# Attention of block 1 in row groups, a recurrence staged across its heads, wider one-hot operations, and moved fills in block 2

## The chip, the cores and the metric

The kernel runs on one core of a Trainium2 chip. The metric is the device time of one execution in microseconds (us). A core has TensorE (PE in the profile, with its weight loads as PEld), VectorE (DVE), ScalarE (ACT), GpSimd (POOL) and the DMA queues, which run beside each other and wait for each other by semaphores.

## What is computed

Two transformer blocks on 512 tokens of width 1024, in float32. Block 1 has a sliding-window attention of 8 heads, a gated linear recurrence (HGRN2) of 4 heads in chunks of 32 tokens, and a PEER layer that picks 16 of 16384 experts per token and head. Block 2 has sparse and latent attention. What the change touches is this much of the reference:

```python
# attention of block 1: window 128, with the block before; one sink logit per head
s = einsum(q, k) * scale - slopes * dist
p = softmax(concatenate([s, sink]))[..., :-1]
o = einsum(p, v)

# recurrence: f = lower_bound + (1 - lower_bound) * sigmoid(f_logit), k = 1 - f
b = cumsum(log(f), axis=2)                   # inside a chunk of 32 tokens
q_dec, k_inv = q * exp(b), k * exp(-b)
o_intra = einsum(where(causal, q_dec @ k_inv, 0), v)
ds = einsum("bnshd,bnshv->bnhdv", k * exp(b_last - b), v)
state = exp(b_last) * state + ds             # chunk after chunk
o_inter = einsum(q_dec, state_before)
o = rms_norm(o_intra + o_inter, g) * silu(hg)

# PEER: two top-16 lists of 128 keys each, the best 16 of their sums, softmax over those
idx = i1 * 128 + i2;  gates = softmax(best)
out = sum over (head, slot) of gate * gelu(u[idx] . h) * v[idx]
```

## The kernel before

Activations lie with the feature on the partitions and 512 tokens in the columns (NT = 4 tiles of 128). Most projections are float32 products made of three matmuls on split operands (`mm3`, L105 to L107: high by high, and two with a low part). A column of such a projection is 8 x 3 = 24 matmuls of 128x512. Its weights arrive by DMA as `raw` and are split into `whi` (ScalarE, L68) and `wlo` (VectorE or GpSimd, L69).

Stages of block 1 are written as generators, and `weave(main, fill, per)` interleaves them: after each `yield` of the main stage it runs columns of the fill until the main stage's count is met. The tile framework then schedules the instructions of each engine by its own estimates, except under `tc.manual_schedule`, where they stay in program order.

Attention (`attention`, L358 on) takes one head at a time: a score matmul (L368; 64 rows of the array, since a head has 64 features) and a bias added by a bf16 matmul with an identity (L370) into a bank `sc`, then `softmax_pt` (VectorE maximum, ScalarE exponential, transposes L175), and the values (L375). Two heads `j` and `j + 4` lie on partitions 0 to 63 and 64 to 127. The fill, `fill_hgrn`, computes the columns q, k, v and gate of the recurrence.

The recurrence (`hgrn`, L454 on) then runs head by head: decayed products on VectorE and ScalarE (L457 to L476), scores and a transpose of the keys (L488, L494), the states of 16 chunks, the outputs (L515, L518), a norm (`hss`, `hr`, `y`) and the turn back (L531). For the states the values are copied into `vb`, which holds for each chunk of a tile its own 32 rows and zeros elsewhere, so that one 128x512 matmul (L503) makes four of them. Their running sum is a chain of 15 operations on VectorE (L507, L509). The fill, `fill_gates`, computes sixteen gate columns, and VectorE also accumulates the adaptive row for block 2 (`mod_junk`).

Behind it the columns `gh` of the two branches are joined (L550) and split for the output projection. In the PEER layer `decode` turns top-16 positions into expert indices and gates for 128 tokens at a time, almost wholly on VectorE, while TensorE already runs the first expert products (`ps_o`, L105 to L107). The three tiles behind the first then have a dense gate table built (`gate_build`): per chunk of OT = 8 tokens, one-hot rows of both index halves (`ohA`, `ohB`), the first multiplied by the gate's three bf16 parts (`ohG`), and three matmuls per token (L931).

In block 2 `fill()` gives the projections that fill its attention: `latents` with norms by a product with ones (L1535), `blocks` with two folds through DRAM (`ab`) and the compressed keys (L1587), `gates_z`, and `heads` (transposes L1633 of `qm`).

## Time and profile before

| | us |
|---|---|
| median of 3 runs (2146.77 to 2150.5) | 2150.09 |
| the profiled execution | 2153.63 |
| its span | 2151.8 |
| TensorE busy | 2039.4 (95%) |
| VectorE busy | 1568.9 (73%) |
| ScalarE busy | 883.4 (41%) |
| GpSimd busy | 495.9 (23%) |

The stages by time in the span: 

| stage | from, to | TensorE busy | VectorE busy |
|---|---|---|---|
| norm and first projections | 0 to 54.6 | 46.89 | 26.14 |
| attention of block 1 | 54.6 to 194.4 | 139.80 | 61.53 |
| recurrence | 194.4 to 359.6 | 158.94 | 121.87 |
| join, output projection | 359.6 to 417 | 51.86 | 33.09 |
| PEER scores | 417 to 560 | 142.87 | 107.63 |
| decode | 560 to 686 | 91.03 | 122.62 |
| gate build | 686 to 853 | 148.13 | 160.69 |
| experts | 853 to 1755 | 900.17 | 708.81 |
| block 2 | 1755 to 2151.8 | 359.74 | 226.57 |

A busy TensorE is not TensorE at its peak, because a matmul's record includes time in which it overlaps its neighbours. Where matmuls of different shapes follow each other, the distance from start to start tells the cost.

### The profile page before, as it was taken

What the parts mean: (1) busy time and instruction counts of PE and PEld (TensorE: products, weight loads), DVE (VectorE), ACT (ScalarE), POOL (GpSimd) and SP (SyncE); (2) the same over time, 40 slices, a digit from 0 to 9 for tenths busy, and PEclk for the clock granted to TensorE, in tenths of its full rate; (3) what the DMA queues carried; (4) which work ended last, traced back from release to release, by engine and by line L of the source; (5) the groups of instructions that cost most, each with busy time, mean ns of one, the idle gap of its engine ahead of it and who ended that gap; (6) DMA issues with size and microseconds to landing.
All of it is one profiled execution on the core that took longest, in us unless ns stands there. A gap on an engine that the chain in (4) does not pass through costs nothing.

```text
span 2151.8 us, 29889 instructions
## 1 busy us (share of the span) xinstructions
PE 2039.4 (95%) x11132; PEld 1724.6 (80%) x11132; DVE 1568.9 (73%) x3139; ACT 883.4 (41%) x1371; POOL 495.9 (23%) x408
## 2 busy tenths in 40 slices
PE   8999999999877899999999999999999999899998
PEld 6777567788776788999999999999988877677776
DVE  4446777559999899687777787888878775446556
ACT  4334434333333677333333333333334453444544
POOL 0000001220334100344444445444422001011000
PEclk9999999999988999999999999999999999899999
DMA  4213334432222555999999989999988761211012
GB/s 153 73 60 118 122 114 127 166 128 85 73 78 69 192 213 204 339 336 321 333 313 327 327 306 331 321 318 327 311 288 295 268 208 34 95 41 59 30 49 79
DMA packets 154376, 410.48 MB, mean 191 GB/s; under 512 B 13789, under 2 KB 63733, under 8 KB 150774
## 3 DMA queue, kind: packets, MB, share of 16 engines
q1 hardware_dynamic: 113332, 247.07, 34.1%
q0 software_dynamic: 37440, 136.33, 18.0%
q10 hardware_dynamic: 3458, 25.17, 3.1%
q8 instruction: 87, 1.43, 0.3%
q14 instruction: 59, 0.48, 0.1%
HBM read 378.64 MB, written 29.37 MB: 190 GB/s over the span
## 4 chain that ended last, share of the span: by engine, by line
PE 77%; DVE 16%; ACT 3%; issue 2%; POOL 1%; DMA 1%; ACTq 0%; DVEq 0%; POOLq 0%
PE ps_mm L105 13%; PE ps_mm L106 13%; PE ps_mm L107 13%; PE ps_o L105 6%; PE ps_o L107 6%; PE ps_o L106 6%; DVE ohG L911 3%; PE ps_tp L106 3%; PE ps_tp L107 3%; PE ps_tp L105 3%; PE ps_o L1325 2%; PE ps_sc L1302 2%; DVE wlo L69 2%; PE ps_tp L1318 1%; DVE ohA L908 1%
## 5 line engine op out<-in xcount | busy, mean ns | idle before, releaser
L68 ACT ACTIVATE whi<-raw 128x1024 fp32r<-128x1024 f32 (+1 forms) x363 | 382.5, 1056 | 626.0 <-issue 371.0
L69 DVE TENSOR_TENSOR wlo<-raw,whi 128x1024 fp32r<-128x1024 f32 (+1 forms) x339 | 415.8, 1229 | 183.9 <-ACT whi L68 183.4
L105 PE MATMUL ps_o<-hT_hi,whi 128*128 128x384 f32 x992 | 344.2, 347 | 18.1 <-ACT act L661 18.1
L107 PE MATMUL ps_o<-hT_hi,wlo 128*128 128x384 f32 x992 | 338.0, 341 | 7.4 <-POOL wlo L69 7.3
L106 PE MATMUL ps_o<-hT_lo,whi 128*128 128x384 f32 x992 | 337.1, 340 | 0.0
L963 POOL DMA_INDIRECT gath<-in_peer_u_dram,idx x128 | 178.7, 1396 | 369.1 <-DVE junk L971 186.0
L963 POOL DMA_INDIRECT gath<-in_peer_v_dram,idx x128 | 176.5, 1379 | 256.6 <-DVE acc L978 213.0
L105 PE MATMUL ps_mm<-hT_hi,whi 128*128 128x512 f32 (+1 forms) x544 | 224.3, 413 | 0.2 <-DVE ga L65 0.2
L107 PE MATMUL ps_mm<-hT_hi,wlo 128*128 128x512 f32 (+1 forms) x544 | 217.5, 400 | 1.0 <-DVE wlo L69 1.0
L106 PE MATMUL ps_mm<-hT_lo,whi 128*128 128x512 f32 (+1 forms) x544 | 216.9, 399 | 0.0
L105 PEld LDWEIGHTS ps_o<-hT_hi,whi 128*128 128x128 f32 x992 | 190.7, 192 | 22.7 <-ACT act L661 19.4
L107 PE MATMUL ps_mm<-whi,wl 128*128 128x512 f32 x512 | 201.2, 393 | 0.0
L106 PE MATMUL ps_mm<-wlo,wh 128*128 128x512 f32 x512 | 200.8, 392 | 0.3 <-DVE wlo L69 0.3
L105 PE MATMUL ps_mm<-whi,wh 128*128 128x512 f32 x512 | 199.4, 389 | 0.4 <-ACT wh L68 0.4
L107 PEld LDWEIGHTS ps_o<-hT_hi,wlo 128*128 128x128 f32 x992 | 190.0, 191 | 8.0 <-POOL wlo L69 7.6
L106 PEld LDWEIGHTS ps_o<-hT_lo,whi 128*128 128x128 f32 x992 | 190.4, 192 | 3.3
L978 DVE SCALAR_TENSOR_TENSOR acc<-gath,w,acc 128x1024 f32<-128x1024 f32 x127 | 162.8, 1282 | 10.4 <-DMA gath<-in_peer_v_dram,idx 8.3
L971 DVE SCALAR_TENSOR_TENSOR junk<-gath,h 128x1024 bf16<-128x1024 f32 x128 | 156.6, 1224 | 14.9 <-DMA gath<-in_peer_u_dram,idx 12.5
L933 ACT ACTIVATE gst<-ps_mm 128x512 f32<-128x512 f32 x96 | 103.4, 1127 | 47.2 <-PE ps_mm L931 45.1
L107 PEld LDWEIGHTS ps_mm<-hT_hi,wlo 128*128 128x128 f32 (+1 forms) x544 | 102.5, 188 | 23.5 <-DVE wlo L69 1.8
L106 PEld LDWEIGHTS ps_mm<-hT_lo,whi 128*128 128x128 f32 (+1 forms) x544 | 102.6, 189 | 22.2 <-issue 3.0
L105 PEld LDWEIGHTS ps_mm<-hT_hi,whi 128*128 128x128 f32 (+1 forms) x544 | 102.8, 189 | 21.1 <-issue 2.8
(482 smaller groups left out, 3611.4 us busy)
## 6 DMA issues: line engine op xcount, KB each, us to landing
raw<-in_peer_uT_dram SPq DMA_DIRECT2D x128, 512.0 KB, 5.4
raw<-in_peer_v_dram SPq DMA_DIRECT2D x128, 512.0 KB, 6.3
raw<-in_w_in_dram SPq DMA_DIRECT2D x59, 512.0 KB, 3.6
gates_dram<-gst ACTq DMA_DIRECT2D x24, 1024.0 KB, 5.4
x<-gates_dram SPq DMA_DIRECT2D x32, 768.0 KB, 9.4
raw<-in_ada_w_dram SPq DMA_DIRECT2D x24, 512.0 KB, 3.7
raw<-in_w_out_dram SPq DMA_DIRECT2D x24, 512.0 KB, 3.4
raw<-in_w_peer_q_dram SPq DMA_DIRECT2D x16, 512.0 KB, 3.6
```

The source lines that it names most:

```text
L68: self.nc.scalar.activation(hi, src, AF.Copy)
L69: (engine or self.nc.vector).tensor_tensor(lo, src, hi.bitcast(F32), op=OP.subtract)
L105: mm(out, a[0], b[0], start=start, stop=False)
L106: mm(out, a[0], b[1], start=False, stop=False)
L107: mm(out, a[1], b[0], start=False, stop=stop)
L911: nc.vector.tensor_tensor(Ag[:, i], A1, pairs(g3T[:, i, cs]), op=OP.mult)
L933: nc.scalar.activation(st[:, :, t0:t0 + 4].rearrange("p a t -> p t a"), p.rearrange("p (t a) -> p t a", t=4), AF.Copy)
L963: nc.gpsimd.indirect_dma_start(out=gath[i], out_offset=None, in_=A["peer_u" if i < NG // 2 else "peer_v"], in_offset=bass.IndirectOffsetOn ...
L971: nc.vector.scalar_tensor_tensor(junk, g, 1.0, h0, op0=OP.mult, op1=OP.mult, accum_out=act0[:, k:k + 1])
L978: nc.vector.scalar_tensor_tensor(acc0, g, w0[:, k:k + 1], acc0, op0=OP.mult, op1=OP.add)
L1302: nc.tensor.matmul(sc[i][:, :n], self.q[i], self.k[i], start=True, stop=False)
L1325: nc.tensor.matmul(self.o(i), self.pt[i][:, kb * 128:(kb + 1) * 128], self.v(i, kb), start=kb == 0, stop=kb == self.tt)
```

## The change

**Attention and its fill.** `Pair` replaces the loop over single heads: both scores stand next to each other, each head on its 64 partitions, then both bias adds; the transposes come one period later, the values one more. TensorE is in program order for the whole stage, so a fill column is an unbroken block of 24. The sigmoids of q and k and the logarithm of the decay move into `fill_hgrn`, and the transposes of `to_tok` come one column later.

```diff
+            nc.scalar.activation(lf, qh, AF.Sigmoid)
+            nc.vector.tensor_tensor(qh, qh, lf, op=OP.mult)
+            nc.scalar.activation(lf, kh, AF.Sigmoid)
             for hh in range(HG_H):
-                to_tok(P, vh[:, hh], col_f())
+                nc.vector.tensor_scalar(lf[:, hh], lf[:, hh], omlb[:, hh:hh + 1], lb[:, hh:hh + 1],
+                                        op0=OP.mult, op1=OP.add)
+                nc.vector.tensor_scalar(kh[:, hh], lf[:, hh], -1.0, 1.0, op0=OP.mult, op1=OP.add)
+            nc.scalar.activation(lf, lf, AF.Ln)
...
+            def scores(self):
+                tt, n = self.tt, self.n
+                sc = [K.bank("sc")[:, :n] for _ in range(2)]
+                for i, hh, ps_ in self.heads:
+                    nc.tensor.matmul(sc[i], qT[ps_, self.j, tt * 128:(tt + 1) * 128],
+                                     kT[ps_, self.k0 * 128:(tt + 1) * 128], start=True, stop=False)
+                for i, hh, ps_ in self.heads:
+                    nc.tensor.matmul(sc[i], K.identb, abias[:, hh, 256 - n:], start=False, stop=True)
...
+            def turn(self):
+                self.pt = []
+                for p in self.p:
+                    tp = K.bank("tp")
+                    for c in range(0, self.n, 128):
+                        nc.tensor.transpose(tp[:, c:c + 128], p[:, c:c + 128], K.ident)
+                    self.pt.append(Q.tile([128, 256], F32, name="sm_pt", bufs=4))
+                    K.copy(self.pt[-1][:, :self.n], tp[:, :self.n])
...
+            def values(self):
+                for i, hh, ps_ in self.heads:
+                    for c in range(self.n // 128):
+                        nc.tensor.matmul(self.o[:, (2 * self.j + i) * 64:(2 * self.j + i + 1) * 64],
+                                         self.pt[i][:, c * 128:(c + 1) * 128], av[:, self.k0 + c, ps_],
+                                         start=c == 0, stop=(c + 1) * 128 == self.n)
...
         def attention():
+            last = None
             for tt in range(NT):
                 o = K.bank("o")
                 for j in range(4):
-                    for g in range(2):
-                        hh = j + 4 * g
-                        ps_ = slice(g * 64, (g + 1) * 64)
-                        k0 = max(tt - 1, 0)
-                        n = (tt + 1 - k0) * 128
-                        sc = K.bank("sc")
-                        nc.tensor.matmul(sc[:, :n], qT[ps_, j, tt * 128:(tt + 1) * 128],
-                                         kT[ps_, k0 * 128:(tt + 1) * 128], start=True, stop=False)
-                        nc.tensor.matmul(sc[:, :n], K.identb, abias[:, hh, 256 - n:], start=False, stop=True)
-                        pt = K.softmax_pt(Q, sc, n, 0.125, sums[:, tt, hh:hh + 1], negm[:, tt, hh:hh + 1],
...
+                    u = Pair(tt, j, o)
+                    u.scores()
+                    yield 2.0
+                    u.turn()
+                    if last:
+                        last.values()
+                    last = u
+            last.values()
...
+        with tc.manual_schedule(engines={nc.tensor.engine}):
+            weave(attention(), fill, 2.0)
```

**The recurrence** becomes `Head` with the steps `prepare`, `scores`, `states`, `outputs` and `turn`, again with TensorE in program order and a fill column after each step; the next head's `prepare` is issued behind a head's `outputs`. The copies into `vb` go: 15 matmuls read 32 rows of `keT` and `vh` each, and write to four banks by their place in the tile. In the join the split of a column comes one column later.

```diff
-                for j in range(4):
-                    js = slice(j * CH, (j + 1) * CH)
-                    if j % 2:
-                        nc.scalar.activation(vb[js, :, j], vh[js, hh], AF.Copy)
-                    else:
-                        nc.vector.tensor_copy(vb[js, :, j], vh[js, hh])
...
+                ds = [K.bank("sc" if j < 2 else "tp") for j in range(4)]
+                for c in range(NC - 1):
+                    tt, j = divmod(c, 4)
+                    js = slice(j * CH, (j + 1) * CH)
+                    nc.tensor.matmul(ds[j][:, tt * 128:(tt + 1) * 128], keT[js, tt], vh[js, hh, tt], start=True, stop=True)
...
-                    ds = K.bank("sc")
-                    nc.tensor.matmul(ds, keT[:, tt], vb[:, tt].rearrange("p a b -> p (a b)"), start=True, stop=True)
...
+        def hgrn(yh):
+            heads = [Head(hh) for hh in range(HG_H)]
+            heads[0].prepare()
+            yield 3.0
...
+                head.scores()
...
+                head.states()
+                yield 1.0
...
+                head.outputs()
+                if after:
+                    after.prepare()
+                yield 1.0
+                head.turn(yh)
...
-                K.split(mh[0][:, c], mh[1][:, c], gh[:, c])
+                if c:
+                    K.split(mh[0][:, c - 1], mh[1][:, c - 1], gh[:, c - 1])
+        K.split(mh[0][:, c], mh[1][:, c], gh[:, c])
```

**Decode and gate build.** The slots of a tile are transposed in the middle of the next tile's top-16 work, an exponential comes later, a reduction becomes a tree of four additions, and the five one-hot operations of a chunk become two wider ones (2 and 3 rows of 1024).

```diff
+                if late and h0 == 0:
+                    turn_slots()
...
-            nc.scalar.activation(e, e, AF.Exp)
...
+            nc.scalar.activation(e, e, AF.Exp)
...
-            pk = RB.tile(kh, F32, name="pk")
-            nc.vector.tensor_reduce(pk, sum1.rearrange("p r k h -> p k h r"), axis=AX.X, op=OP.add)
+            pk = sum1[:, 0]
+            for n in (8, 4, 2, 1):
+                nc.vector.tensor_tensor(sum1[:, :n], sum1[:, :n], sum1[:, n:2 * n], op=OP.add)
...
-            nc.vector.tensor_tensor(A1, iota, pairs(i1T[:, cs]), op=OP.is_equal)
-            nc.vector.tensor_tensor(B, iota, pairs(i2T[:, cs]), op=OP.is_equal)
-            for i in range(3):
-                nc.vector.tensor_tensor(Ag[:, i], A1, pairs(g3T[:, i, cs]), op=OP.mult)
...
+            nc.vector.tensor_tensor(hot.rearrange("p c j e i -> p (c j) e i"),
+                                    iota_e[:, None].to_broadcast([128, 2 * pr, PK, 2]),
+                                    ikT[:, ch].rearrange("p c (j i) -> p (c j) i", i=2)[:, :, None]
+                                    .to_broadcast([128, 2 * pr, PK, 2]), op=OP.is_equal)
+            nc.vector.tensor_tensor(Ag, hot[:, 0:1].to_broadcast([128, 3, pr, PK, 2]),
+                                    g3T[:, ch].rearrange("p c (j i) -> p c j i", i=2)[:, :, :, None]
+                                    .to_broadcast([128, 3, pr, PK, 2]), op=OP.mult)
```

**Block 2.** The norms of the latents come behind the first fold, one z column ahead of the compressed keys, and the turn of `qm` one tile later.

```diff
+                    if kv == 0:
+                        late["norms"]()
+                        yield 1.0
+                yield from z_col(late["z"][0], 0)
...
-                    qm = T.tile([128, 4, 96], F32, name="qm", bufs=2)
+                    qm = T.tile([128, 4, 96], F32, name="qm", bufs=3)
...
-                    if len(turns) > 1:
+                    if len(turns) > 2:
```

Three places of the order of instructions follow. The first is TensorE in the attention with full windows. Before, a pair's first transposes and values are set singly between projection matmuls (`ps_mm`):

```order
L175 MATMUL ps_tp<-ident,sm_p 128x128 x2
L107 MATMUL ps_mm<-hT_hi,wlo 128x512
L175 MATMUL ps_tp<-ident,sm_p 128x128 x2
L105 MATMUL ps_mm<-hT_hi,whi 128x512
L375 MATMUL ps_o<-av,sm_pt 128x64 x2
L106 MATMUL ps_mm<-hT_lo,whi 128x512
L375 MATMUL ps_o<-av,sm_pt 128x64 x2
L107 MATMUL ps_mm<-hT_hi,wlo 128x512
L105 MATMUL ps_mm<-hT_hi,whi 128x512
```

Now one period of the stage, with the pair's work in one piece (transposes of the newest pair, values of the one before it, scores of the next):

```order
L107 MATMUL ps_mm<-hT_hi,wlo 128x512
L392 MATMUL ps_tp<-ident,sm_p 128x128 x4
L399 MATMUL ps_o<-av,sm_pt 128x64 x4
L373 MATMUL ps_sc<-kT,qT 128x256 x2
L376 LDWEIGHTS identb
L376 MATMUL ps_sc<-ga,identb 128x256
L376 LDWEIGHTS identb
L376 MATMUL ps_sc<-ga,identb 128x256
L105 MATMUL ps_mm<-hT_hi,whi 128x512
```

Transposes and values of both heads now stand together, and the projections on either side are unbroken. The second place is TensorE in the second head of the recurrence. Before, state matmuls (L503) and outputs (L515, L518) are mixed with projections:

```order
L518 MATMUL ps_o<-st,qd 32x128
L515 MATMUL ps_o<-vh,at 128x128
L503 MATMUL ps_sc<-vb,keT 128x512
L518 MATMUL ps_o<-st,qd 32x128 x2
L105 MATMUL ps_mm<-y_hi,whi 128x512
L106 MATMUL ps_mm<-y_lo,whi 128x512
L518 MATMUL ps_o<-st,qd 32x128
L107 MATMUL ps_mm<-y_hi,wlo 128x512
L518 MATMUL ps_o<-st,qd 32x128
L515 MATMUL ps_o<-vh,at 128x128
```

Now the fifteen state matmuls, alternating between two kinds of banks, follow a block of 24 projections, and the outputs follow the next block:

```order
L107 MATMUL ps_mm<-hT_hi,wlo 128x512
L543 MATMUL ps_sc<-vh,keT 128x128 x2
L543 MATMUL ps_tp<-vh,keT 128x128 x2
L543 MATMUL ps_sc<-vh,keT 128x128 x2
L543 MATMUL ps_tp<-vh,keT 128x128 x2
L543 MATMUL ps_sc<-vh,keT 128x128 x2
L543 MATMUL ps_tp<-vh,keT 128x128 x2
L543 MATMUL ps_sc<-vh,keT 128x128 x2
L543 MATMUL ps_tp<-vh,keT 128x128
L105 MATMUL ps_mm<-y_hi,whi 128x512
```

Nothing stands between the state matmuls. The third place is VectorE from the first head's sum of squares (`hss`) to its normed output `y`, for which the turn's transposes wait. Before:

```order
L524 TENSOR_REDUCE hss<-sq 128x4
L126 TENSOR_SCALAR rs_v<-hss 128x4
L69 TENSOR_TENSOR wlo<-raw,whi 128x1024
L1131 SCALAR_TENSOR_TENSOR mod_junk,mod_acc<-raw,csil 128x1024
L129 RECIPROCAL rs_r<-rs_t 128x4
L137 TENSOR_TENSOR rs_t<-rs_r 128x4
L138 TENSOR_TENSOR rs_t<-rs_t,rs_v 128x4
L139 TENSOR_SCALAR rs_t<-rs_t 128x4
L140 TENSOR_TENSOR hr<-rs_r,rs_t 128x4
L528 TENSOR_TENSOR y<-ps_o,hr 128x512
```

Now the same piece holds work of the next head:

```order
L567 TENSOR_REDUCE hss<-sq 128x4
L502 TENSOR_TENSOR qd<-qh,e 128x512
L126 TENSOR_SCALAR rs_v<-hss 128x4
L510 TENSOR_TENSOR e<-b 128x512
L506 TENSOR_TENSOR ki<-kh,e 128x512
L495 SCALAR_TENSOR_TENSOR b<-scm,lf 128x512
L129 RECIPROCAL rs_r<-rs_t 128x4
L1200 SCALAR_TENSOR_TENSOR mod_junk,mod_acc<-raw,csil 128x1024
L137 TENSOR_TENSOR rs_t<-rs_r 128x4
L138 TENSOR_TENSOR rs_t<-rs_t,rs_v 128x4
L139 TENSOR_SCALAR rs_t<-rs_t 128x4
L140 TENSOR_TENSOR hr<-rs_r,rs_t 128x4
```

and right behind these, up to the turn's output `yf`:

```order
L514 TENSOR_TENSOR ke<-kh,e 128x512
L571 TENSOR_TENSOR y<-ps_o,hr 128x512
L69 TENSOR_TENSOR wlo<-raw,whi 128x1024
L579 SCALAR_TENSOR_TENSOR yf<-ps_tp,gh_col,hgs 128x512
L69 TENSOR_TENSOR yh_lo<-yf,yh_hi 128x512
```

Behind `hss` now stand the next head's products (`qd`, `e`, `ki`, `b`, `ke`), which stood behind `yf` before.

## Rows read from the trace of the kernel before

**Rows 1.** The chain of work that ended last, shares by engine.
```profile
PE 77%; DVE 16%; ACT 3%; issue 2%; POOL 1%; DMA 1%; ACTq 0%; DVEq 0%; POOLq 0%
```

**Rows 2.** Windows: busy time and instructions of each engine, granted clock, DMA share, GB/s.
```profile
260.00:280.00 20.00, 18.18 (x67) 9.56 (x67) 14.24 (x27) 4.00 (x6) 0.00 (x0) 0.83 0.33 105
611.00:661.00 50.00, 39.13 (x193) 37.62 (x192) 48.94 (x191) 15.27 (x23) 19.28 (x8) 0.86 0.27 84
736.00:786.00 50.00, 44.77 (x477) 39.59 (x476) 50.00 (x80) 37.01 (x40) 0.00 (x0) 1.00 0.61 221
1865.00:1875.00 10.00, 7.42 (x70) 7.16 (x70) 1.69 (x5) 0.71 (x1) 0.00 (x0) 0.66 0.29 79
```

**Rows 3.** TensorE in time in block 1: start, duration, instructions; two successive pairs.
```profile
102.21 0.70 PE L368 MATMUL ps_sc<-kT,qT 64*128 64x256 f32 x2
...
110.83 0.70 PE L368 MATMUL ps_sc<-kT,qT 64*128 64x256 f32 x2
```

**Rows 4.** TensorE in time in block 2: one attention unit and its projections.
```profile
1892.99 1.00 PE L1325 MATMUL ps_o<-vn,sm_pt 128*128 128x64 f32 x8
...
1894.36 0.70 PE L1302 MATMUL ps_sc<-kn,qn 64*128 64x256 f32 x4
...
1895.09 0.48 PE L105 MATMUL ps_mm<-hT_hi,whi 128*128 128x512 f32 x1
1895.41 0.39 PE L106 MATMUL ps_mm<-hT_lo,whi 128*128 128x512 f32 x1
...
1898.63 1.00 PE L1325 MATMUL ps_o<-vn,sm_pt 128*128 128x64 f32 x8
```

**Rows 5.** Window of line 105, the first matmul of each projection trio.
```profile
194.40:359.60 165.20, 65.20 (x156) 29.48 (x156) 0.98 0.41 127
```

**Rows 6.** TensorE in time, the fourth head of the recurrence.
```profile
333.32 1.13 PE L488 MATMUL ps_sc<-qd,ki 128*128 128x128 f32 x8 [0.19 <-DVE ki L468]
...
350.55 0.38 PE L515 MATMUL ps_o<-vh,at 128*128 128x128 f32 x2
...
353.18 0.43 PE L518 MATMUL ps_o<-st,qd 128*32 128x128 f32 x8
```

**Rows 7.** VectorE by line and shape, 222 to 356: busy us, mean ns, idle.
```profile
L509 DVE SCALAR_TENSOR_TENSOR st<-st,dec,ps_sc 128x128 f32<-128x128 f32 x56 | 19.4, 346 | 1.6
...
L457 DVE TENSOR_TENSOR_SCAN b<-scm,lf 128x512 f32<-128x512 f32 x3 | 3.6, 1215 | 0.0
...
L528 DVE TENSOR_TENSOR y<-ps_o,hr 128x512 f32<-128x512 f32 x3 | 2.1, 691 | 0.1
...
L137 DVE TENSOR_TENSOR rs_t<-rs_r 128x4 f32<-128x4 f32 x3 | 0.5, 159 | 0.0
```

**Rows 8.** What TensorE waited for: us in total, times, longest.
```profile
PE ps_o L105 <- ACT act L661: 18.1, 4, 9.1
...
PE ps_tp L1633 <- DVE qm L1154: 5.9, 2, 5.1
PE ps_mm L1587 <- DMA ab<-abx: 4.8, 1, 4.8
...
PE ps_mm L105 <- DVE gh L550: 4.5, 5, 1.4
...
PE ps_tp L1535 <- ACT sq L1529: 1.8, 1, 1.8
```

**Rows 9.** VectorE by line and shape, the decode, 561 to 686.
```profile
L825 DVE TENSOR_REDUCE pk<-sum 128x128 f32<-128x2048 f32 x4 | 15.4, 3842 | 0.1
...
L846 DVE TENSOR_TENSOR ge<-ge,step 128x2048 bf16<-128x2048 bf16 x4 | 13.1, 3269 | 0.1
...
L819 DVE TENSOR_TENSOR ge<-at,row_at 128x2048 bf16<-128x2048 bf16 x4 | 4.9, 1218 | 0.0
```

**Rows 10.** VectorE in time in the gate build, a chunk from its first operation.
```profile
722.31 0.69 DVE L908 TENSOR_TENSOR ohA<-iota_e,i1T 128x1024 bf16<-128x1024 bf16 x1
...
725.32 0.69 DVE L908 TENSOR_TENSOR ohA<-iota_e,i1T 128x1024 bf16<-128x1024 bf16 x1
```

238 lines of the change are left out of this document (125 added, 113 removed).

## The prediction

> **What bounds the kernel now.** I read the chain of work that ended last first, because it says which engine an edit must relieve: TensorE carries 77% of it, VectorE 16% [rows 1]. So time saved on TensorE counts nearly everywhere. The stretches show where that fails [rows 2]: in the decode VectorE is busy 48.94 of 50 us, in the gate build all of 50.00 while TensorE has 44.77. There only VectorE work counts. Two more stretches hold idle TensorE time and a lower clock: 260 to 280 (18.18 of 20 us, clock 0.83) in the recurrence, and 1865 to 1875 (7.42 of 10, clock 0.66) in block 2. These are means over TensorE's two levels, 2.4 GHz (1.0) and 1.2 (0.5), and both follow a wait of the engine. After that I read the order of TensorE's instructions where the change moves them, and last its list of waits for what stands still.
>
> **1. Attention of block 1.** In the old order one pair of heads takes from 102.21 to the next pair's 110.83, 8.62 us [rows 3], with 24 projection matmuls. A projection matmul's step is (1898.63 - 1895.41) / 14 = 0.23 us [rows 4], so 5.52 are projections and 3.10 are the pair and the switches it causes. Block 2 already has an attention unit in the new form: values, transposes, scores side by side, masks, then an unbroken block [rows 4]. It takes 1895.09 - 1892.99 = 2.10 us, and the first matmul behind it 0.32 instead of 0.23, so 2.19. The gain of the side-by-side form can be seen in one shape: one head's two records of 64x256 last 0.70 us in all [rows 3], and two heads' four records, on two row groups, 0.70 as well [rows 4]. Block 1's bias add has 256 columns against the mask's 128, so I add 0.1: 2.29 a pair, a gain of 0.81. Twelve pairs give 9.7. For the four pairs of the first token tile, which have half the transposes and values, I take 0.6 each, 2.4. **-12 us.** Bounds: -8, if the sigmoids and the logarithm that now stand on ScalarE among the softmaxes make TensorE wait; -14, if the switch costs vanish wholly. Those gates cost TensorE nothing as long as a pair's softmax has the 5.5 us block as cover.
>
> **2. Recurrence.** The stretch 194.4 to 359.6 lasts 165.2 us and holds 156 first matmuls of projections [rows 5], so 468 with the other two of each trio, or 107.6 us at 0.23. The other 57.6 are the heads' own matmuls, switches and stalls. What a head needs in unbroken form: its scores and transposes as now, some 1.5 (1.13 for eight records, [rows 6]); its outputs 353.18 - 350.55 plus about 0.4 = 3.0, since the fourth head already issues them so [rows 6]; the turn 0.6; four switches 0.4. The states change form: four 128x512 matmuls on masked copies become 15 of 32 rows, dealt round to four row groups and four banks. That is 30 records of 128 columns. Without overlap they would cost what a score record costs, about 1.13/8 = 0.14, so 4.2 us; with overlap by two, as [rows 3] against [rows 4] show, 2.1. I take 2.4, nearer the overlap that the two-group row shows. Sum 7.9 a head, 31.6 for four, so the stage could give back 26.
>
> It will not give all of it, because TensorE's order is now fixed, with a block of 24 projections (5.5 us) between steps. The turn of a head waits for y. The new VectorE order puts the next head's preparation between that head's sum of squares and its y: six operations of 0.69 us (L528's size), a scan of 1.2, an accumulating step of 1024 columns for the adaptive row of 1.2 (sized as in part 4), and six small ones of 0.16 [rows 7]. That is 7.5 us, with ScalarE's square of the same 512 columns ahead, some 0.6: 2.6 late on head one. On head two gate multiplications of 0.69 stand there too, so I take 5; on head three 1; head four prepares nothing. Together 9. The state chain has 14 steps of 0.35 [rows 7], with a granule split of 1.2, a copy and an adaptive-row step between them: 8.3 against 5.5 of cover plus the states' own 2.4, so 0.5 a head, 2. Idle time lowers the clock in this stretch already (0.83 at 260 to 280, 0.17 of 18.18 busy, 3 us), and I leave those 3. Late in all: 14 to 15. **-11 us**; bounds 0 (every new wait twice as long) and -22 (waits covered).
>
> **3. The join behind it.** TensorE waits 4.5 us, five times, for the gated column that VectorE writes [rows 8]. Splitting each column one column later takes that off ScalarE's and VectorE's way. **-2.5**, bounds 0 and -4.
>
> **4. Decode.** Two waits of TensorE go: for ScalarE's act, 18.1 us, whose longest (9.1) arises while ScalarE stands at an exponential that VectorE has not fed, and which the change puts behind more VectorE work [rows 8]. As VectorE is full, I count nothing for them; they only let weights arrive earlier. What counts is VectorE's own: four reductions of 3.84 us [rows 9] become trees of four additions of 1024, 512, 256 and 128 columns. A 512-column operation takes 0.69 [rows 7]; a double-size one costs twice that less the fixed part of 0.16 (part 5): 1.22 + 0.69 + 0.42 + 0.29 = 2.6. That is 1.2 a tile, 5 in all. Against it stands GpSimd, which splits weights at the same time: the same 128x2048 size takes 1.22 in one row and 3.27 in another, with two full inputs [rows 9]. The long one I read as held off by a split. A reduction has one input; the tree's additions have two, so a split that used to hide under the reduction may now hold one up by 2 us a tile. But the exponential no longer holds ScalarE, so splits also spread into the top-16 phases. **-6**, bounds -10 and +5.
>
> The Trainium skill, in "SBUF — State Buffer" (section "SBUF: two separate sides"), says that a VectorE operation with two SBUF inputs and a GpSimd operation lock each other out for a whole instruction. The 3.27 us row agrees with it, and by that rule the tree would be the worse form wherever a split runs.
>
> **5. Gate build.** A chunk of eight tokens now has five one-hot operations of 128x1024: 725.32 - 722.31 = 3.01 us [rows 10], a step of 0.602 for operations that last 0.69, so neighbours overlap by 0.09. A 128x2048 operation of the same type takes 1.218 [rows 9], against 2 x 0.69 for two halves: 0.16 saved, 0.07 of it in the step, as one overlap is lost too. One 2048-wide and one 3072-wide operation then step at 1.13 and 3 x 0.602 - 2 x 0.07 = 1.67, 2.80 a chunk. 384 tokens make 48 chunks: 0.21 x 48. **-10**, bounds -5 (TensorE at 44.77 of 50 is the next engine [rows 2]) and -10.5.
>
> **6. Block 2.** Three waits are addressed [rows 8]: 4.8 us of L1587 for a DMA, 5.9 of L1633 for qm (longest 5.1), 1.8 of L1535 for the squares. A z column (24 matmuls, 5.5 us) now stands ahead of L1587, the norms come behind the first fold, and qm may run two tiles ahead. The DMA wait goes, 4.8; behind it the stretch 1865 to 1875 ran at clock 0.66, worth 0.34 of 7.42 busy, 2.5; the norms give 1.8; of qm I count 4. The transposes behind the folded hidden layer lose the cover of a column and wait for ScalarE: 1.5 back. **-12**, bounds -5 and -17.
>
> Sum: -12 - 11 - 2.5 - 6 - 10 - 12 = -53.5. The profiled execution took 2153.63 us (its span 2151.8), 3.5 above the median 2150.09 of the runs shown. 2153.6 - 53.5 = 2100.1 for such an execution, **2097** against the median.
>
> **The rivals.**
> A: The stalls of fixed order eat the recurrence's gain, and the trees lose their cover. For it: the 7.5 us of VectorE work between sum and y, against a 5.5 block. Parts 1, 3, 5 and 6 remain, -36.5, with +3 for decode: about 2117.
> B: The row groups do not overlap, so the change does not do what it says. Scores stay at 0.63 a head (+0.6 x 12 for the large pairs, +0.3 x 4 for the small, so +8) and the states cost 4.2 (+1.8 x 4 = 7). 2097 + 15 = 2112. Against it: the 0.70 us of [rows 3] and [rows 4].
> C: More overlap and full cover: states at 4.2 / 4 = 1.1, waits of the recurrence hidden, -22 there, and decode -10: 2082.
> The Trainium skill, in "TensorE: Matmul & The Clock Gate" (section "Measured speedup vs the span model"), gives 3.07x for four 32-row tiles. By that figure the states would cost 4.2 / 3.07 = 1.4 us a head, an estimate; no row of this kernel has four row groups.
> D, slower: the wide one-hots with their longer access pattern fall to half the pace. A float32 operation of 512 columns takes 0.69 [rows 7], the bf16 one of 1024 the same [rows 10], so the bf16 form moves two elements where f32 moves one. At f32's pace 5120 columns cost about 10 x 0.6 - 0.5 = 5.5 us a chunk, +2.5 x 48 = 120, less the 43.5 of the other parts: about 2227. It decides from 3.01 + 43.5/48 = 3.9 us a chunk on. Against it: innermost, the pattern is the same pair of elements as before.
>
> **How the numbers follow.** Forecast with its own range 2080 to 2110: 0.52. A 0.22, B 0.10, C 0.10, D 0.04, and 0.02 for anything else that makes it slower. 0.2% (4.3 us) is about what a measurement of this kernel can tell from no change. A with the worst bounds of its other parts (-8, 0, -5, -5, +5) ends at 2137, still faster; I give "same" 0.03 from that tail, faster 0.91, slower 0.06. For 8 in 10 the range takes in A, B and most of C: 2078 to 2125.
>
> **What would show it.** Right: pairs of 7.8 us in place of 8.6; 15 state matmuls in 2 to 3 us; TensorE waits for y of 2 to 5 us in the recurrence; chunks at 2.80 us; the wait for ab gone. Wrong: one-hots above 1.3 and 1.9 us, or a recurrence stretch that is not shorter, or decode tiles on VectorE as long as before. Because VectorE writes y in its program order, the first thing I would look at is the wait of the turn's transposes.

## The result: 24 us faster, less than half of the forecast

The changed kernel takes **2126.09 us** (median of 4, 2123.56 to 2128.35) against 2150.30 for the kernel before (2146.77 to 2150.83): a ratio of 0.9891, 95% interval 0.9873 to 0.9908. The forecast was 2097, range 2078 to 2125. The profiled execution took 2125.71. This is the top of its page (span; busy time by engine; shares of the chain that ended last):

```profile
span 2123.9 us, 29904 instructions
...
PE 2007.9 (95%) x11220; PEld 1723.1 (81%) x11220; DVE 1558.1 (73%) x2998; ACT 883.4 (42%) x1368; POOL 489.7 (23%) x408
...
PE 81%; DVE 12%; ACT 3%; DMA 2%; issue 2%; POOL 1%; ACTq 0%; DVEq 0%; POOLq 0%
```

TensorE's share of the chain rose from 77 to 81% and VectorE's fell from 16 to 12% [rows 1], so TensorE is even more the engine to relieve. To see where the 28 us of span came from, I compared the same instructions in both traces, each time the first or the last of its kind, and took the time from one to the next:

| piece, from and to | before | after | difference | forecast |
|---|---|---|---|---|
| start to end of attention (first turn of `yo`) | 190.41 | 179.57 | -10.8 | -12 |
| recurrence, to the first projection of `yh` | 169.22 | 168.70 | -0.5 | -11 |
| join, to the last product `gh` | 30.74 | 30.18 | -0.6 | -2.5 |
| PEER scores and decode, to the first one-hot | 295.94 | 295.33 | -0.6 | -6 |
| gate build, to its last matmul | 169.52 | 161.17 | -8.4 | -10 |
| experts, to the last accumulating step | 841.48 | 844.79 | +3.3 | 0 |
| block 2, from the first score of a head to the last | 251.02 | 240.71 | -10.3 | -12 |

The other pieces differ by less than 0.2. The recurrence holds the largest miss. In the list of what TensorE waits for (us in total, times, longest), these are new:

```profile
PE ps_mm L1000 <- ACT gst L1002: 11.2, 10, 1.1
PE ps_o L561 <- DVE st L550: 10.2, 13, 1.6
...
PE ps_tp L577 <- DVE y L571: 5.0, 2, 4.7
...
PE ps_mm L105 <- ACT qm L1717: 3.5, 1, 3.5
```

L561 and L577 are the recurrence's outputs and turn, L1000 the gate build, L1717 block 2. The wait for `ab` is gone [rows 8].

**Attention** does what was forecast. In the order of time on TensorE (start, duration, instructions), two successive pairs of block 1 start 7.72 us apart, where they were 8.62 apart [rows 3] and 7.8 was forecast:

```profile
103.88 0.70 PE L373 MATMUL ps_sc<-kT,qT 64*128 64x256 f32 x4
111.60 0.70 PE L373 MATMUL ps_sc<-kT,qT 64*128 64x256 f32 x4
```

A later pair shows its inside. Both heads' scores are one row of four records and 0.70 us, the two bias adds start 0.64 behind its start, and the projections go on 0.79 behind it:

```profile
146.21 0.70 PE L373 MATMUL ps_sc<-kT,qT 64*128 64x256 f32 x4
146.85 0.39 PE L376 MATMUL ps_sc<-ga,identb 128*128 128x256 bf16 x2
147.00 0.48 PE L105 MATMUL ps_mm<-hT_hi,whi 128*128 128x512 f32 x1
```

**The recurrence** gains what its new form gives and loses it again. TensorE in the first head: fifteen state matmuls (the pieces below belong to one unbroken row of them), then the outputs:

```profile
204.19 0.38 PE L543 MATMUL ps_sc<-vh,keT 32*128 32x128 f32 x2
204.20 0.38 PE L543 MATMUL ps_tp<-vh,keT 32*128 32x128 f32 x2
...
205.09 0.27 PE L543 MATMUL ps_tp<-vh,keT 32*128 32x128 f32 x1
205.29 0.50 PE L105 MATMUL ps_mm<-hT_hi,whi 128*128 128x512 f32 x1
...
211.84 1.19 PE L561 MATMUL ps_o<-st,qd 128*32 128x128 f32 x22
214.18 0.79 PE L561 MATMUL ps_o<-st,qd 128*32 128x128 f32 x4 [1.15 <-DVE st L550]
```

The states start at 204.19 and the projections go on at 205.29, so the states take 1.1 us, where 2.4 was forecast. The outputs begin as a block: 22 records in 1.19 us. Then each needs the next state, and a piece with 4 records takes 0.79 us behind a wait of 1.15. VectorE, which makes the states, shows why (the bracket is idle time ahead and its releaser):

```profile
207.53 1.23 DVE L1200 SCALAR_TENSOR_TENSOR mod_junk<-raw,csil 128x1024 bf16<-128x1024 f32 x1 [1.14 <-DMA raw<-in_ada_w_dram]
...
208.68 0.29 DVE L548 COPY st<-ps_sc 128x128 f32<-128x128 f32 x1
...
212.63 1.23 DVE L1200 SCALAR_TENSOR_TENSOR mod_junk<-raw,csil 128x1024 bf16<-128x1024 f32 x1
...
218.27 0.69 DVE L567 TENSOR_REDUCE hss<-sq 128x4 f32<-128x512 f32 x1 [1.13 <-ACT sq L565]
...
224.40 0.69 DVE L571 TENSOR_TENSOR y<-ps_o,hr 128x512 f32<-128x512 f32 x1
```

Ahead of the first state copy VectorE stands at `mod_junk`, a step of the adaptive row for block 2, because its weights have not arrived; in the middle of the chain stands another such step. From the sum of squares to `y` it is 224.40 - 218.27 = 6.1 us. Over the stage VectorE's waits for these loads alone come to 18.4 us (us in total, times, longest), and in the kernel before, in the second row, to 5.6:

```profile
DVE mod_junk L1200 <- DMA raw<-in_ada_w_dram: 18.4, 11, 3.8
```

```profile
DVE mod_junk L1131 <- DMA raw<-in_ada_w_dram: 5.6, 8, 1.4
```

Two windows in which TensorE waits, for `y` (4.7 us) and for states, show the clock (TensorE's busy time stands behind the window's length; the last three numbers are the granted clock, the DMA share and GB/s):

```profile
255.00:265.00 10.00, 5.26 (x23) 4.08 (x22) 7.45 (x15) 3.73 (x5) 0.00 (x0) 0.84 0.24 61
...
325.00:335.00 10.00, 7.76 (x22) 5.28 (x23) 6.11 (x18) 2.08 (x3) 0.00 (x0) 0.56 0.53 180
```

A clock of 0.56 is close to the lower of its two levels.

**Decode** does not shorten. VectorE by line and shape (busy us, mean ns, idle):

```profile
L891 DVE TENSOR_TENSOR sum<-sum 128x1024 f32<-128x1024 f32 x4 | 13.2, 3298 | 0.1
L912 DVE TENSOR_TENSOR ge<-ge,step 128x2048 bf16<-128x2048 bf16 x4 | 9.0, 2245 | 0.1
...
L891 DVE TENSOR_TENSOR sum<-sum 128x512 f32<-128x512 f32 x4 | 4.9, 1234 | 0.1
...
L891 DVE TENSOR_TENSOR sum<-sum 128x256 f32<-128x256 f32 x4 | 3.8, 945 | 0.1
...
L891 DVE TENSOR_TENSOR sum<-sum 128x128 f32<-128x128 f32 x4 | 3.2, 811 | 0.1
```

The additions cost 3.30 + 1.23 + 0.95 + 0.81 = 6.29 us a tile in the mean, where 2.6 was forecast and the reduction took 3.84 [rows 9]. These means mix two cases. The addition of 512 columns takes 0.69 in three of the four tiles, the first one here, and 2.86 in the last:

```profile
L891 DVE TENSOR_TENSOR sum<-sum 128x512 f32<-128x512 f32 x1 | 0.7, 692 | 0.0
...
L891 DVE TENSOR_TENSOR sum<-sum 128x512 f32<-128x512 f32 x1 | 2.9, 2861 | 0.0
```

The long one starts at 661.10, beside a split on GpSimd:

```profile
661.04 2.37 POOL L69 TENSOR_TENSOR wlo<-raw,whi 128x1024 fp32r<-128x1024 f32 x1 [1.07 <-ACT whi L68]
```

In the same way the additions of 256 and 128 columns take 0.42 and 0.29 except in one tile each, with 2.50 and 2.37 beside a split. The addition of 1024 columns meets a split in all four tiles. The multiplication that had 3.27 in the mean [rows 9] has 3.29 and 3.24 in two tiles, beside splits, and 1.23 in the two others, where none runs; its mean is 2.25.

**A gate-build chunk** in VectorE's order of time takes 724.33 - 721.40 = 2.93 us in place of 3.01 [rows 10]; 2.80 was forecast:

```profile
721.40 1.22 DVE L974 TENSOR_TENSOR hot<-iota_e,ikT 128x2048 bf16<-128x2048 bf16 x1
722.65 1.76 DVE L978 TENSOR_TENSOR ohG<-hot,g3T 128x3072 bf16<-128x3072 bf16 x1
724.33 1.22 DVE L974 TENSOR_TENSOR hot<-iota_e,ikT 128x2048 bf16<-128x2048 bf16 x1
```

**Block 2**: the compressed keys (L1663) run without the wait for `ab`, but TensorE stands 2.04 us at the next step:

```profile
1852.75 2.18 PE L1663 MATMUL ps_mm<-w,ab 128*62 128x128 f32 x32
1856.96 0.30 PE L1672 MATMUL ps_mm<-ident,hid 128*128 128x128 f32 x1 [2.04 <-issue]
```

### The profile page after: what moved, and what is told of

The parts are those of the page before. It is cut to its first block, busy times and chain, and to the rows that moved or that the text cites. A ratio compares the mean times of both kernels' runs of the same rounds, so it can differ in the third digit from the quotient of the medians.

```text
span 2123.9 us, 29904 instructions
## 1 busy us (share of the span) xinstructions
PE 2007.9 (95%) x11220; PEld 1723.1 (81%) x11220; DVE 1558.1 (73%) x2998; ACT 883.4 (42%) x1368; POOL 489.7 (23%) x408
## 4 chain that ended last, share of the span: by engine, by line
PE 81%; DVE 12%; ACT 3%; DMA 2%; issue 2%; POOL 1%; ACTq 0%; DVEq 0%; POOLq 0%
PE ps_mm L105 13%; PE ps_mm L106 13%; PE ps_mm L107 13%; PE ps_o L105 7%; PE ps_o L107 6%; PE ps_o L106 6%; PE ps_tp L107 3%; PE ps_tp L106 3%; PE ps_tp L105 3%; PE ps_mm L1000 2%; PE ps_o L1394 2%; PE ps_sc L1371 2%; PE ps_tp L1387 1%; DVE wlo L69 1%; DVE sum L891 1%
```

## The experiments

The expectations call "theory 1" what I held after the comparison: the recurrence's own work shrank as forecast, and the steps of the adaptive row in VectorE's fixed stream, above all their waits for loads (1a), delay the states and `y`; TensorE waits, and its clock falls. The rivals stand with each run. Stage times below are from the first turn of `yo` to the first projection of `yh`, as in the table.

**1. The recurrence in its old order, the rest of the change kept.**

```diff
-        with tc.manual_schedule(engines={nc.tensor.engine}):
-            weave(hgrn(yh), fill, 1.0)
...
+        weave(hgrn(yh), fill, 1.0)
...
```
with the body of `hgrn` as it was (the copies `vb`, 128x512 state matmuls).

> The changed kernel with the recurrence of before (head by head, masked value copies, TensorE's order free), its gates still beside the attention. Theory 1 (the new recurrence's gain on TensorE was eaten by its own waits for VectorE and by the lower clock they bring): the restaging is worth about 1 us net, since the join began 12.1 us earlier than before and the attention alone explains 10.8 of them; so 2125 to 2129 us against 2126.1 of the changed kernel. Rival (the restaging does give its 11 us and the moved gates cost about as much): 2137 us.

Measured: 2115.53 us (2111.16 to 2119.47), ratio 0.9832 (0.9809 to 0.9855). Both expectations missed. The stage takes 154.2 us, 14.5 less than in the changed kernel, and 15 less than in the kernel before, whose code it is. So restaging cost some 10 us here, and something else in the change made the old order fast. Runs 6 and 11 to 14 come back to this.

**2. The adaptive row out of the stage.** Its 24 steps go into the fill of the attention.

```diff
+        ada = modulation(K, P, csil)
...
-            ada = modulation(K, P, csil)
...
-                next(ada)
...
```
The lines taken out stand in `fill_gates`; `next(ada)` now stands behind the columns of `fill_hgrn`.

> The changed kernel with the 24 accumulating steps of the adaptive row (1024 columns each, one DMA wait each) moved from the recurrence to the attention's fill; nothing else moves. Theory 1 (VectorE's order makes the waits: these steps and their DMA stand inside the state chain and ahead of y): TensorE's waits for the states fall from 10.2 us to under 3, the wait for y from 5.0 to about 3, the clock of the recurrence rises above 0.95, total 2110 to 2118 us. Rival, theory 2 (TensorE's fixed order with one column of cover is too short for any VectorE order): waits stay above 10 us together, total 2123 to 2128. Either way the attention may lose 0 to 3 us, as VectorE is busy less than half of it.

Measured: 2101.42 us (2097.31 to 2105.53), ratio 0.9775 (0.9750 to 0.9799), better than either expectation. The stage takes 137.6 us; the attention ends 1.0 later. TensorE's waits there:

```profile
PE ps_tp L580 <- DVE y L574: 2.8, 2, 2.3
...
PE ps_o L564 <- DVE st L553: 1.4, 2, 1.0
```

and the windows of the stage, this kernel's first (granted clock third from the right) and the changed kernel's second:

```profile
180.00:320.00 140.00, 135.72 (x854) 111.00 (x854) 93.77 (x178) 61.23 (x76) 0.61 (x3) 1.00 0.25 76
```

```profile
180.00:350.00 170.00, 154.82 (x845) 119.60 (x844) 115.22 (x219) 60.33 (x75) 0.62 (x3) 0.92 0.41 124
```

The 31 us are waits (10.2 + 5.0 against 1.4 + 2.8, 11 us) and, for the rest, the same matmuls running slower, at a mean clock of 0.92 in place of 1.00 and with outputs that come in small pieces. Steps from one projection to the next cost 8.5 us less in all, the outputs' own steps 11.4 less (sums over the stage, from start to start with waits taken out).

**3. VectorE in program order too, the next head's preparation one column later.**

```diff
+                yield 1.0
                 if after:
                     after.prepare()
-                yield 1.0
...
-        with tc.manual_schedule(engines={nc.tensor.engine}):
+        with tc.manual_schedule(engines={nc.tensor.engine, nc.vector.engine}):
```

> The changed kernel with the next head's preparation issued behind the column that follows the outputs, and VectorE in program order in the recurrence, so that y comes before the preparation and the state chain is unbroken; the adaptive row's steps stay in the stage. Theory 1: the wait for y (5.0 us) goes and the waits for states fall below 5, total 2113 to 2121 us. Theory 2: new waits of the scores for ki take their place, together still above 12 us, total 2124 to 2130.

Measured: 2243.91 us (2240.59 to 2248.77), ratio 1.0439 (1.0414 to 1.0464). Both expectations missed, and the stage takes 280.3 us. The waits for states and `y` vanish, but TensorE now waits for split weights, and VectorE for TensorE's columns:

```profile
PE ps_mm L107 <- DVE wlo L69: 97.6, 18, 10.9
```

```profile
DVE gh L65 <- PE ps_mm L107: 37.6, 5, 10.8
```

In program order the split of a column's weights stands behind the copy of the column before it and an adaptive step, so each engine waits for the other (VectorE 94 us in all for finished columns). For the loads of the adaptive row it does not wait once. The run changed another thing than it was made to test, and says nothing on the loads.

**4. The one reduction back in place of the tree.**

```diff
-            pk = sum1[:, 0]
-            for n in (8, 4, 2, 1):
-                nc.vector.tensor_tensor(sum1[:, :n], sum1[:, :n], sum1[:, n:2 * n], op=OP.add)
+            pk = RB.tile(kh, F32, name="pk")
+            nc.vector.tensor_reduce(pk, sum1.rearrange("p r k h -> p k h r"), axis=AX.X, op=OP.add)
```

> The changed kernel with one reduction (before: 3.84 us) in place of the tree of four additions in the decode. Theory (the additions have two inputs and are held up by GpSimd's splits, which used to hide under the reduction: the first addition takes 3.30 us where the size needs 1.22): the decode shortens by 4 to 8 us in all, total 2118 to 2122. Rival (a split holds up some two-input operation wherever it falls, so the tree merely has the bad luck): no change, 2125 to 2128.

Measured: 2129.85 us (2124.69 to 2132.47), ratio 0.9903 (0.9878 to 0.9928). In the trace the one-hots start 4.0 us earlier than in the changed kernel: the reduction takes 3.86 us a tile as before, the later multiplication still 2.24. So the tree is the worse form, by 4 us, and the shorter multiplication belongs to the rest of the edit. The total doesn't show it: from the experts' last step to the last score of block 2 this profile takes 7.4 us longer (below).

**5. Each load of the adaptive row requested one step ahead.**

```diff
+    nxt = K.fetch(A["ada_w_2"][0])
...
-        w = K.fetch(A["ada_w_2"][j])
+        w, nxt = nxt, K.fetch(A["ada_w_2"][j + 1]) if j < 23 else None
```

> The changed kernel with the adaptive row's steps where they are, but each load issued one step earlier. In the changed kernel VectorE stands 18.4 us in the recurrence, 11 times, at an adaptive-row step whose weights have not landed, with the state chain and y behind it. Theory 1a (that DMA wait is what the states wait for, not the step's 1.2 us of work): VectorE's wait for these loads falls under 5 us, TensorE's waits for states from 10.2 to under 5, total 2106 to 2116 us. Theory 1b (the work of 20 steps, 24 us of VectorE, in the wrong places): waits for states stay at 6 to 10 us, total 2118 to 2126.

Measured: 2125.75 us, ratio 0.9888 (0.9867 to 0.9908): no change. VectorE still waits 19.0 us, 12 times, for the loads, so the edit did not take the wait away, and the run does not tell 1a from 1b. A load needs a free buffer of `raw`, of which there are four, shared with the weights of the projections; the DMA queue's own list of waits has 49.4 us for splits (`wlo`), 20.9 for states and 14.1 for adaptive steps, all on VectorE. That this is why the earlier request changed nothing fits these waits; it was not tested.

**6. The recurrence's gates back at its start, in the new order.**

```diff
-            nc.scalar.activation(lf, qh, AF.Sigmoid)
...
+        nc.scalar.activation(lf, qh, AF.Sigmoid)
```

> The changed kernel with the recurrence's sigmoids, products and logarithm back at the start of the recurrence. Run e1 showed that the old recurrence is 15 us shorter with these gates beside the attention than in the kernel before. Theory (moving the gates is worth that much by itself, because at the stage's start they use up the projections that cover the heads): 2136 to 2146 us. Rival (in the new order the stage is held by its own waits whatever its start): 2124 to 2130.

Measured: 2132.68 us, ratio 0.9922 (0.9897 to 0.9947). The stage takes 168.5, the attention ends where it did. In the stage, the gates' place is worth nothing in the new order; the profiled execution loses 5.0 us against the changed kernel, all of it in block 2 (below).

**7. Each score followed by its own bias add (a single time).**

```diff
                     nc.tensor.matmul(sc[i], qT[ps_, self.j, tt * 128:(tt + 1) * 128],
                                      kT[ps_, self.k0 * 128:(tt + 1) * 128], start=True, stop=False)
-                for i, hh, ps_ in self.heads:
                     nc.tensor.matmul(sc[i], K.identb, abias[:, hh, 256 - n:], start=False, stop=True)
```

> The changed kernel with each head's score matmul followed by its own bias add, so that two heads' scores no longer stand next to each other; everything else of the pair stays in one piece. Theory (row groups overlap: 0.64 us for both heads' scores against 0.63 for one): a pair takes about 0.6 us longer, the attention 12 x 0.6 + 4 x 0.3 = 8 us longer, 2134 in one look. Rival (the gain is the unbroken order alone): under 2 us longer.

Measured: 2147.19. The attention stage lasts 135.84 us, against 125.16 in the changed kernel and 135.73 before, all with 384 or 386 projection matmuls. One head's score alone lasts 0.70, and the next head's starts 0.84 later:

```profile
152.91 0.70 PE L373 MATMUL ps_sc<-kT,qT 64*128 64x256 f32 x2
...
153.75 0.70 PE L373 MATMUL ps_sc<-kT,qT 64*128 64x256 f32 x2
```

So the row groups side by side are the whole gain of the attention, and the unbroken blocks give nothing net without them: against the kernel before, the steps of run 7's projections shrink by 7.5 us, but those of its transposes and values grow by 4.8, and waits of 2.5 come in. Of the 21 us by which the total exceeds the changed kernel's, 10 lie behind the experts (below).

**8. Runs 2 and 4 together.**

> The changed kernel with the adaptive row's steps in the attention's fill (e2, 2101.4 us) and one reduction in the decode (e4, whose trace showed the decode 4 us shorter though its total did not). Theory: the two add, 2096 to 2099 us. Rival (the 4 us are given back behind the decode, in stages that DMA or the clock sets): 2100 to 2103.

Measured: 2098.46 us (2090.40 to 2102.28, 5 executions), ratio 0.9753 (0.9731 to 0.9775). That is inside the 2096 to 2099 expected if the two add. It is the fastest kernel of this study by its median, though not apart from run 2, so the total cannot tell the theory from its rival.

**9. The adaptive steps stay, their loads go.** Each step reads a weight granule that is already there.

```diff
-        w = K.fetch(A["ada_w_2"][j])
+        w = K.last.bitcast(F32)
```

> The changed kernel with the adaptive row's steps left in the recurrence, but reading a weight granule that is in place already, so their loads and the wait for them go and the work of VectorE stays. It leaves out the adaptive row's true values: its time alone is read. Run e5 could not take the wait away (VectorE still stood 19.0 us at these loads, since the load waits for a buffer that VectorE frees). Theory 1a (the wait for the loads holds the state chain and y): TensorE's waits for states fall from 10.2 us to under 4, the recurrence's time beside projections from 60 to 30 to 40 us, total 2098 to 2110. Theory 1b (the 24 us of work in wrong places is enough): waits for states stay at 7 to 10 us, total 2116 to 2126.

Measured: 2105.92 us (2103.88 to 2107.84), ratio 0.9789 (0.9760 to 0.9817). The stage takes 144.7: of the 31 us, 24 go with the loads and 7 with the steps themselves. TensorE still waits 2.3 us for states and 4.4 for `y`. What goes with the loads are VectorE's waits for them and the buffers of `raw` that they hold; the two were not taken apart.

**10. Five one-hot operations as before, on the new layout (a single time).**

> The changed kernel with the five one-hot operations of 1024 columns in place of the two wide ones; tiles as in the changed kernel. Theory (the wide forms save 0.2 us a chunk, but a third of it is given back, since the experts' first weights come by a DMA that does not start earlier): gate build 9.5 to 10 us longer, TensorE's wait of 2.1 us behind it down to 0.4 as before, 6 to 7 us longer in all. Rival (the wait behind it has another cause): all 9.5 to 10 us are lost.

Measured: 2138.52. VectorE in time, a chunk from its first operation:

```profile
722.17 1.28 DVE L981 TENSOR_TENSOR hot<-iota_e,ikT 128x1024 bf16<-128x1024 bf16 x2
723.38 1.89 DVE L983 TENSOR_TENSOR ohG<-hot,g3T 128x1024 bf16<-128x1024 bf16 x3
725.18 1.28 DVE L981 TENSOR_TENSOR hot<-iota_e,ikT 128x1024 bf16<-128x1024 bf16 x2
```

A chunk takes 3.01 again, and the gate build (first one-hot to last matmul) 165.1 us, 3.9 more than in the changed kernel, which is 48 x 0.08. So the wide forms give 3.9 of the 8.4 us, and both expectations (9.5 to 10) missed. The other 4.5 are there without them, and they lie in the first eight chunks. There, in the kernel before, a GpSimd split takes 14.4 us, TensorE waits 7.3 us for it, and VectorE 5.8 for TensorE:

```profile
PE ps_o L107 <- POOL wlo L69: 7.3, 1, 7.3
```

The changed kernel and run 10 have neither wait; their longest split there takes 3.45 and 2.45 us.

**11. Run 1 with the adaptive row early, and 12. Run 1 with the gates late.**

> Run e2 (adaptive row's steps in the attention's fill, 2101.4 us) with the old recurrence of run e1. Theory (the restaging's own gain on TensorE is real, some 8 us on the state matmuls and more on the outputs, once VectorE lets it through): 2110 to 2116 us, and the recurrence's time beside projections 40 to 45 us against 29 of e2. Rival (the adaptive row is all there is to it, and the old recurrence gains as much by its removal): 2099 to 2104.

> The recurrence in its old order, as in the run with the old recurrence, but the gates' sigmoids, logarithm and multiplications back at its start in place of beside the attention. Theory: the gates' place alone explains why the old order took 154.2 us in that run and 169.2 in the kernel before, so the stage is 165 to 171 us long here (from the yo turn to the first output projection of yh) and the kernel takes 2128 to 2133 us. Rival: the 15 us come from something else that changed around the stage (the attention's program order, the column blocks in its fill, the split of the join); then the stage stays at 153 to 158 us and the kernel takes 2114 to 2120.

Measured: run 11 2109.17 us (2107.80 to 2111.03), ratio 0.9805 (0.9777 to 0.9833), stage 149.0; run 12 2111.28 (2108.77 to 2113.55), ratio 0.9803 (0.9776 to 0.9830), stage 152.5. With the adaptive row in the stage the new order costs 14.5 us against run 1; without it the new order gains 11.4 (137.6 against 149.0). Run 12 refutes the guess that the gates' place had made the old order fast.

**13 and 14. The outputs in one piece or mixed with projections.** The code of the old recurrence is the same in both; with this edit of the gates ahead of it (another buffer for `lf`, the output gate's sigmoid first) the scheduler orders TensorE in another way.

```diff
+        lf = P.tile([128, HG_H, S], F32, name="lf")
...
-        lf = T.tile([128, HG_H, S], F32, name="lf")
+        nc.scalar.activation(gh[:, :HG_H], hgs, AF.Sigmoid)
+        nc.vector.tensor_tensor(hgs, hgs, gh[:, :HG_H], op=OP.mult)
...
-        nc.scalar.activation(lf, hgs, AF.Sigmoid)
-        nc.vector.tensor_tensor(hgs, hgs, lf, op=OP.mult)
```

Run 13 is the kernel before with this edit, run 14 is run 12 without it.

> The kernel before with one edit: the buffer lf lies in the outer pool and the sigmoid of the output gate goes to gh and stands first. The computation is the same. In this kernel's order of TensorE the outputs of a head stand in one piece (3 places where a projection is followed by an output, in place of 24). Theory: the mixture of outputs and projections is what made the recurrence 169.2 us in the kernel before, and whole outputs, which the edit of lf brings, are why the old recurrence inside the change takes 152 to 154. Then the stage takes 152 to 157 us here, the output matmuls' own steps fall from 13.5 to about 7 us, and the kernel takes 2134 to 2139 us. Rival: the order of outputs costs little and the attention stage ahead of it made the difference; then the stage stays at 165 to 170 us and the kernel within 2146 to 2152.

> The reverse of the run before it: the change with the old recurrence and the gates at its start, and lf back in the inner pool as in the kernel before; then 25 places have a projection followed by an output. Theory (order of the outputs): the stage goes back from 152.5 to 165 to 171 us, the kernel to 2123 to 2129. Rival (the attention stage ahead of it): the stage stays at 151 to 156 us, the kernel at 2109 to 2114.

Measured: run 13 2137.49 us (2130.78 to 2141.62), ratio 0.9933 (0.9911 to 0.9955), stage 151.7; run 14 2129.68, ratio 0.9890 (0.9859 to 0.9921), stage 167.3. The stage follows the outputs' order both times. Output matmuls in run 13, and then in run 14:

```profile
223.06 0.42 PE L518 MATMUL ps_o<-st,qd 128*32 128x128 f32 x8
223.41 0.49 PE L515 MATMUL ps_o<-vh,at 128*128 128x128 f32 x2
```

```profile
228.39 0.41 PE L551 MATMUL ps_o<-st,qd 128*32 128x128 f32 x2
228.73 0.50 PE L106 MATMUL ps_mm<-hT_lo,whi 128*128 128x512 f32 x1
```

The next matmul starts 0.35 us behind eight records in a row, and 0.34 behind two that stand alone. The eight go to four groups of columns and overlap. Set singly among projections, each pair costs what the eight cost. Of the 17.5 us by which run 13 shortens the stage, these steps are 6.7; the rest are waits (4.3, above all for `ki`), steps of projections (3.5) and of state matmuls (2.9). That these too follow from the order of the outputs is not shown: the edit moves the start of the stage as well.

**What block 2 adds to every comparison.** Its code is the same in the changed kernel and in all runs but 13. Yet from its first score to its last it takes 240.7 (the changed kernel) to 247.9 us (runs 1, 7, 8, 10, 14), with a middle value of 245.9 over these 14 profiles; the old code takes 251.0 and 250.8 (run 13). The same stretch of work (85 records of TensorE), in the changed kernel and in run 1:

```profile
1983.46:2003.46 20.00, 15.73 (x85) 10.85 (x84) 10.99 (x20) 12.22 (x23) 0.00 (x0) 0.83 0.09 27
```

```profile
1974.99:1997.25 22.26, 18.61 (x85) 13.10 (x84) 10.98 (x20) 12.21 (x23) 0.00 (x0) 0.69 0.08 25
```

The clock is 0.83 in one and 0.69 in the other, and run 1 takes 2.3 us longer, though the waits of this stage are nearly the same lists. The piece between the experts' last step and the first of these scores varies too, from 113.6 to 117.0 us. So the total of a run carries up to some 10 us that I cannot put down to its edit, and where edits are small I compare stages, not totals.

## Why the prediction was wrong

**The step that failed is part 2, the recurrence.** Its sum of the heads' own work was near and on the safe side: 26 us to give back if nothing waits; run 2, with the row gone, gave 31.6 against the kernel before. What failed is "Late in all: 14 to 15", made of 9 for `y`, 2 for the chain of states and 3 for the clock. I priced VectorE's operations, the adaptive steps among them at 1.2, and never asked whether their data are there. VectorE waited 18.4 us for the loads, and the stage became 168.7 - 137.6 = 31 us longer than without the row. Run 9 shows 24 of it to go with the loads, against the mere steps' 7. Term by term: the wait for `y` was 5.0, not 9; the wait for states 10.2, not 2, because steps of the row stand inside their chain; and the 3 for the clock became 20 against run 2, namely 8.5 of slower projections and 11.4 of outputs that came in pieces, a cost that I had put at nothing.

In the old form no output waits for a state, mixed or whole, and VectorE waits less for these loads (5.6 us in the kernel before, 8.5 in run 12); why the loads come so much later in the new order was not tried apart. The kernel before paid elsewhere: its outputs' steps took 13.5 us (sum from start to start) against 6.8 when whole (13.6 and 6.8 in runs 14 and 13). I read the mixed outputs in the order of instructions and put them under "switches and stalls"; that a reorder within the old form (runs 13 and 14) goes with 15 to 17 us, I did not see. Against that version (run 12, 152.5) the restaging as made loses 16.

**Rival A named the right place** (2117: the recurrence gains nothing, the trees lose their cover), but gave the other four parts 36.5 us, and they came to 30.1, of which the experts' stage took back 3.3. C was right on the states (1.1 us: four row groups overlap almost fully) and wrong on the waits. The Trainium skill's 3.07 ("TensorE: Matmul & The Clock Gate", section "Measured speedup vs the span model") would give 1.4 us, an estimate; the trace has 1.1. B and D fell: scores overlap (run 7), and the wide one-hots keep their pace of 1.22 and 1.76 us.

**The rest, by parts.** 1, attention: -10.8 for -12, with the mechanism shown by run 7. 3, join: -0.6 for -2.5; the wait for `gh` went from 4.5 to 4.0 only, in five waits as before; VectorE's first product there still waits for ScalarE's sigmoid. 4, decode: -0.6 for -6, of which the working itself gives only 5. The sizes were right where no split runs (0.69, 0.42 and 0.29); the collision that I put in the bound (+2 us a tile) was the rule, with 6.29 - 3.84 = +2.45 a tile, and run 4 prices the tree at +4 us net. The Trainium skill's rule in "SBUF — State Buffer" (section "SBUF: two separate sides"), cited in the prediction, agrees: the 512-column addition takes 2.86 us beside a split and 0.69 without one. 5, gate build: 8.4 for 10, near by luck: the chunk saves 0.08, not 0.21, since `ohG`, which reads what `hot` has just written, starts 1.25 us behind it, not 1.13. Wide forms are worth 3.9 (run 10), and the 4.5 from the start of the stage, where a wait for a split is gone, I had not forecast. 6, block 2: -10.3 in the profiled pair, which is luck too: -5 for the middle of 14 profiles, at the lower bound; the wait for `ab` gave way to 2.0 at L1672 and 3.5 for a bank that `qm` holds.

**The 3.3 us behind the gate build** need not be the change's. Run 13 has the code of before there, and takes 844.0 us against 841.5. It has a wait of 1.1 us for `wh`, and behind it this window:

```profile
855.57:865.57 10.00, 10.00 (x43) 8.75 (x43) 8.30 (x12) 4.71 (x7) 2.74 (x2) 0.83 0.94 350
```

Run 12, which has the changed gate build, waits 0.5 there, keeps the clock, and takes 841.8:

```profile
838.98:848.98 10.00, 10.00 (x51) 8.95 (x50) 8.15 (x13) 4.64 (x8) 2.74 (x2) 1.00 0.94 350
```

The other 13 profiles, of the changed kernel and its variants, take 843.7 to 845.5. What decides between a wait of 0.5 and of 1.1 us there stays open, as does which short wait in block 2 starts its lower clock.

## What to carry to other kernels

Before you fix TensorE's order, list for each wait that it can meet everything that stands ahead of the awaited instruction on its engine, and for each of those whether it waits for a DMA: loads that nobody needs soon, consumed in the middle of a dependent chain, cost 24 us here. Matmuls that fill only part of the array's rows or columns are to stand side by side, since a lone pair costs as much as eight; the order is worth more than the form. Where short waits move the clock, judge a small edit by its stage and by several kernels, as one profile of a stage can lie 7 us from the next.

## What was not expected of the hardware

Fifteen matmuls of 32 rows on four row groups and four banks took 1.1 us, about a quarter of the 4.2 estimated for a serial run, and output matmuls on four column groups overlapped as well: the next matmul starts 0.35 us behind eight records and 0.34 behind two. A VectorE addition of 512 columns with two inputs took 0.69 us alone and 2.86 beside a GpSimd split. An operation of VectorE that reads its predecessor's output starts 1.25 us behind it (duration 1.22), while independent ones overlapped by 0.09 [rows 10]. In the slices of 10 us that are shown with, or just behind, waits of some 1 to 5 us, the granted clock was 0.56 to 0.84; in the recurrence the slower projections (8.5 us) cost almost as much as the waits themselves (11).
